# Joint of the output stage and the second MLP: group two's first 24 products placed in the gap, a group's two feature blocks multiplied first and both ReLUs after, the last cast later

## Chip, core and metric

The kernel runs on one core of one Trainium2 chip. The metric is the device time of one execution in microseconds, as the median of several runs. A core has five engines with a queue each, and each queue is worked off in order: TensorE (PE, with its weight loads shown apart as PEld), VectorE (DVE), ScalarE (ACT), GpSimd (POOL) and SyncE (SP), which issues the DMAs. An instruction waits until the instructions of other engines that it depends on have signalled; whatever stands behind it in its queue waits with it.

## What is computed

Two layers over 512 latent tokens and 256 context tokens of width 1024. Each layer is a token mixer (pooling in the first, grouped-query attention in the second) and then a squared-ReLU MLP with 4096 hidden features. The change lies where the attention of layer two ends and its MLP begins, on latent tokens alone:

```python
y_lat = attention(...) @ w_o
x = x + gt1 * rms_norm(y_lat, g_mix_post)
h = rms_norm(x, g_mlp_pre) * (1.0 + sc2) + sh2
m = jnp.square(jax.nn.relu(h @ w_in)) @ w_out      # w_in 1024 x 4096, w_out 4096 x 1024
x = x + gt2 * rms_norm(m, g_mlp_post)
```

## The kernel before

Every fp32 operand of a product is split into a high part (a cast to the matmul's format, on ACT) and a low part (source minus high part, on DVE). A product is then three matmuls: high by high, high by low, low by high. "A product" below means one such matmul instruction on PE; 128 rows of the depth of 1024 are called a step `k`, so that one block of 128 hidden features over some tokens takes 8 steps of 3 products, 24 in all.

**Output stage** (`output`). It multiplies the attention's result by `w_o` for four tiles of 128 tokens, each in two column halves (`attn_mm`, PSUM tiles `psy`, L1302). `attn_ev` multiplies the result by the gate (DVE, L326) and takes the mean square (ACT, L170); POOL turns it into a reciprocal root (`rstd`, L183 and L185); `norm_r` adds the residual (DVE, L329); `norm_s` takes the mean square of the new rows (ACT, L170, then POOL L177 and L185) and `norm_c` scales them (ACT L526 or DVE L528). When two tiles are scaled, `norm_pair` (`modulated_pair`) transposes them on PE (L350, PSUM tiles `psx`), modulates them (DVE L358, ACT L361) and splits them into `h1H` in `ra` and `h1L` in `unit[0]`, which is part of `rb`. The first pair (tiles 0 and 1) is split in two pieces of four steps `k` each (ACT L369, DVE L370), the second pair (tiles 2 and 3) in four pieces of two steps (ACT L364, DVE L365). The stage also computes the last gate from `w_ada` on DVE (`ada_sum`, L268 to L277).

**Second MLP** (`mlp1`). The 4096 hidden features are worked in 16 groups of 256; here they are counted one to sixteen, while the code counts `g` from 0. `Inner.part(c, f, ks)` issues the products (L567) of feature block `f` (0 or 1) of a group for the token chunk `c` and the steps `ks`, into a PSUM tile `psin` taken from the pool `psA`, which has two buffers of two banks each. `squares` multiplies a block, takes its ReLU and then its square (ACT L578 and L912), block after block. Of two groups each the squares are combined and multiplied by `w_out` in seven products of sums, a fast scheme (`product`, PSUM tiles `pso` from the pool `psB`, L921); the weight sums and the operands are made by `put` and `both` (ACT L893, DVE L893 and L899).

Group one is already joined to the output stage before the change: the token half of the first pair (chunk 0, 24 products per block, 256 tokens wide) is multiplied inside `output`, the other half in `mlp1`. Its blocks take one `psA` buffer each, with one bank per token half. Group two is multiplied in `mlp1` in 48 products that are 512 tokens wide; its weights are loaded during the output stage and split whole (ACT L142, DVE L145) at the start of `mlp1`.

**What sets the order.** The steps of `output` carry a due time (`at(time, function, ...)`) and are issued in the order of these times; the framework then schedules the instructions of each engine by its own timing model, except for those that are pinned with `keep_in_program_order`. So the place of an instruction in a queue follows from the due times and from that model together. The loads of weights go through three buffers `raw` (pool `rawp`): a load is issued when an earlier content of a buffer has been read for the last time.

## Time and profile before

| | us |
|---|---|
| median of 3 runs | 1172.9 (1172.45 to 1174.26) |
| the profiled execution | 1173.48 |
| its span on the core | 1171.7 |
| PE busy in the span | 1143.0 |
| DVE busy | 938.4 |
| ACT busy | 636.7 |
| POOL busy | 67.0 |

The span is what the profile covers; the execution took 1.8 us more. A row of the timeline gives start, duration, engine, line, operation, output and inputs with their shapes, and in brackets how long the engine had been idle and what ended that. Matmuls overlap in the array, so a row's duration (0.28 us for one that is 256 wide) is longer than the distance to the next one. Rows that follow each other with the same text are merged, with their number behind an x. Times are counted from the start of the span.

### The profile page before, as it was taken

To read this page: it belongs to the slowest core of one execution; us is meant where nothing else is said; L and a number is where in the kernel's file an instruction comes from. 1 tells how busy PE (TensorE), PEld (TensorE's weight loads), DVE (VectorE), ACT (ScalarE), POOL (GpSimd) and SP (SyncE) were. 2 spreads that over 40 slices of the span, in tenths; PEclk is the share of its full clock that TensorE was granted. 3 is DMA by queue.
4 is the path that set the end of the run, shared out by engine and by line. 5 is a ranking of instruction groups with operands and counts; after the bars stand their busy time and mean duration, and the time that the engine had idled before them with its cause. 6 is when DMAs were issued, how large, how long until landed. Compare 5 with 4: busy or idle time off the path is not lost.

```text
span 1171.7 us, 15966 instructions
## 1 busy us (share of the span) xinstructions
PE 1143.0 (98%) x6172; PEld 989.2 (84%) x6172; DVE 938.4 (80%) x1538; ACT 636.7 (54%) x1082; POOL 67.0 (6%) x120
## 2 busy tenths in 40 slices
PE   7899999999999999999999999999899999999997
PEld 5579899889899988998887889988888888888886
DVE  4688687989988997996778599877787779778876
ACT  4577655555454534555675388852776436535522
POOL 2030000000000000000241200001100000000001
PEclk9899999999999999999999999999999999999999
DMA  9884213343334334343423101115234124314312
GB/s 375 354 318 154 72 45 135 133 159 109 144 144 144 144 137 147 112 144 108 180 73 107 37 1 37 37 73 197 91 138 150 61 84 144 108 36 144 108 37 107
DMA packets 25516, 147.32 MB, mean 126 GB/s; under 512 B 2785, under 2 KB 5217, under 8 KB 9698
## 3 DMA queue, kind: packets, MB, share of 16 engines
q1 hardware_dynamic: 25442, 146.32, 34.2%
q8 instruction: 48, 0.79, 0.3%
q14 instruction: 26, 0.21, 0.1%
HBM read 138.96 MB, written 7.34 MB: 125 GB/s over the span
## 4 chain that ended last, share of the span: by engine, by line
PE 49%; issue 42%; POOL 3%; DVE 2%; ACT 2%; DMA 1%; SPq 0%; POOLq 0%; DVEq 0%; ACTq 0%
PE pso L817 22%; PE psin L691 18%; PE psin L567 3%; PE psq L1064 2%; PE pspool L65 1%; POOL rs L185 1%; PE psada L65 1%; PE pspool L490 1%; POOL rs L1073 1%; DMA raw<-in_w_ada 1%; DMA xr<-in_x 1%; PE psada L227 1%; POOL ms L183 1%; DVE ra L65 0%; ACT junk L170 0%
## 5 line engine op out<-in xcount | busy, mean ns | idle before, releaser
L817 PE MATMUL pso<-units,rb 128*128 128x512 f32 x1152 | 278.2, 392 | 0.0
L817 PEld LDWEIGHTS pso<-units,rb 128*128 128x128 f32 x1152 | 214.8, 188 | 41.2
L273 DVE SCALAR_TENSOR_TENSOR rows<-raw,cond,rows 128x256 f32<-128x256 f32 x280 | 126.5, 475 | 2.0
L829 DVE TENSOR_TENSOR acc<-acc,pso 128x512 f32<-128x512 f32 x129 | 85.1, 674 | 41.4 <-PE pso L817 41.2
L567 PE MATMUL psin<-ra,rb 128*128 128x512 f32 (+1 forms) x432 | 103.3, 340 | 1.8 <-ACT ra L364 1.6
L921 PE MATMUL pso<-units,pairs 128*128 128x512 f32 x336 | 82.3, 389 | 0.0
L567 PE MATMUL psin<-ra 128*128 128x512 f32 x256 | 80.5, 390 | 0.0
L567 PEld LDWEIGHTS psin<-ra,rb 128*128 128x128 f32 x432 | 69.9, 189 | 11.3 <-ACT ra L364 1.9
L921 PEld LDWEIGHTS pso<-units,pairs 128*128 128x128 f32 x336 | 63.1, 188 | 13.1
L925 DVE TENSOR_TENSOR acc<-acc,pso 128x512 f32<-128x512 f32 x72 | 48.7, 681 | 28.8 <-PE pso L921 28.8
L183 POOL TENSOR_SCALAR ms<-ss 128x1 f32<-128x1 f32 x20 | 11.4, 572 | 998.3 <-ACT junk L170 946.1
L691 PE MATMUL psin<-ra,units 128*128 128x384 f32 x336 | 65.5, 337 | 0.4 <-ACT psin L703 0.4
L691 PE MATMUL psin<-sums,units 128*128 128x384 f32 x336 | 63.9, 337 | 0.0
L691 PEld LDWEIGHTS psin<-ra,units 128*128 128x128 f32 x336 | 59.7, 188 | 3.9 <-ACT psin L703 0.9
L691 PEld LDWEIGHTS psin<-sums,units 128*128 128x128 f32 x336 | 58.9, 188 | 1.7
L145 DVE TENSOR_TENSOR units<-raw,units 128x1024 fp32r<-128x1024 f32 (+2 forms) x49 | 55.1, 1148 | 4.5 <-ACT units L142 4.4
L567 PEld LDWEIGHTS psin<-ra 128*128 128x128 f32 x256 | 48.0, 188 | 10.0
L142 ACT CAST units<-raw 128x1024 fp32r<-128x1024 f32 (+2 forms) x49 | 46.8, 994 | 14.0 <-PE pso L817 10.2
L827 ACT COPY acc<-pso 128x512 f32<-128x512 f32 x48 | 27.2, 588 | 48.9 <-PE pso L817 48.6
L567 PE MATMUL psin<-rb 128*128 128x512 f32 (+1 forms) x144 | 52.6, 367 | 0.2 <-DVE rb L365 0.2
L1064 PE MATMUL psq<-units,ra 128*128 128x512 f32 x216 | 51.7, 392 | 0.0
L567 PE MATMUL psin<-rb,ra 128*128 128x512 f32 x128 | 49.8, 389 | 0.0
(279 smaller groups left out, 2346.7 us busy)
## 6 DMA issues: line engine op xcount, KB each, us to landing
raw<-in_w_ada SPq DMA_DIRECT2D x48, 1024.0 KB, 4.9
raw<-in_w_mlp_in SPq DMA_DIRECT2D x32, 1024.0 KB, 4.9
raw<-in_w_mlp_out SPq DMA_DIRECT2D x32, 1024.0 KB, 5.3
raw<-in_w_qkv SPq DMA_DIRECT2D x6, 1024.0 KB, 4.8
spill<-xr SPq DMA_DIRECT2D x10, 512.0 KB, 4.2
xr<-spill SPq DMA_DIRECT2D x10, 512.0 KB, 6.8
raw<-in_w_o SPq DMA_DIRECT2D x4, 1024.0 KB, 4.8
xr<-in_x SPq DMA_DIRECT2D x4, 512.0 KB, 5.2
```

What stands on the lines that cost most here:

```text
L65: return lambda *args, **kw: self.tc.keep_in_program_order(f(*args, **kw))
L142: a = sc.copy(hi, raw)
L145: b = ve.tensor_tensor(out=lo, in0=raw, in1=hi, op=ALU.subtract)
L273: ve.scalar_tensor_tensor(out=r, in0=raw[:, k, :], scalar=cond[:, k, c:c + 1], in1=r, op0=ALU.mult, op1=ALU.add)
L567: te.matmul(ps[:, bank, o:o + ln], w[:, k, fs], rhs, start=start, stop=(k == KT - 1 and n == 2), skip_group_check=len(ks) < KT)
L691: te.matmul(bank, w[k], a[k], start=start and k == 0 and m == 0, stop=stop and k == 3 and m == 2, skip_group_check=True)
L817: te.matmul(pss[h][:, 0:cols[h][1]], a[:, f, ts_], w[:, f, cols[h][0]:sum(cols[h])], start=(n == 0 and not seeded[t]), stop=(n == len(seq) ...
L827: sc.copy(d, ps)
L829: ve.tensor_tensor(out=d, in0=d, in1=ps[:, 0:w], op=ALU.add)
L921: te.matmul(ps, a, w, start=(m == 0), stop=(m == len(seq) - 1))
L925: ve.tensor_tensor(out=M[n][:, t], in0=M[n][:, t], in1=ps, op=ALU.add)
L1064: te.matmul(ps, a[:, k, sl], w[:, k % 4, :], start=(k == 0 and n == 0), stop=(k == KT - 1 and n == 2))
```

## The change

Five things change together.

1. *Both blocks of groups one and two share one PSUM buffer* (`paired`): block `f` takes bank `f`, and the two token halves lie beside each other in that bank. Group one then holds one of the two `psA` buffers, and group two can take the other one while group one is still being multiplied.
2. *Group two is multiplied in token halves of 256.* The 24 products of its first block over the first half (`first1[1].part(0, 0, ...)`, due at 47.5 and 47.6) are issued in the output stage.
3. *Its weights are split in halves.* The raw weights were loaded in the output stage before, too. Now the first block's half is cast and subtracted there (`half_early`, due at 36, L1339 and L1340) into `rb[4096:6144]`, and the second block's half at the start of `mlp1`.
4. *`squares` of a paired group* issues the products of both blocks that are still open, and then the two ReLUs and squares.
5. *The last cast of the first token pair* (steps 4 to 7) with its subtraction leaves `modulated_pair` and becomes `upper_half`, due at 41.65 (L1386 and L1387), with the cast pinned. Group one's products on that half are issued in pieces of four steps.

```diff
-    def modulated_pair(t, i, s, hi, lo, works, wide, fine, on_act):
+    def modulated_pair(t, i, s, hi, lo, works, wide, fine, on_act, late=None):
...
                 h = works[q // 2].rearrange("p (k n) -> p k n", n=256)
+                if late is not None and q == 3:
+                    late.append((place(hi, ks), place(lo, ks), h))
+                    continue
                 sc.copy(place(hi, ks), h)
                 ve.tensor_tensor(out=place(lo, ks), in0=h, in1=place(hi, ks), op=ALU.subtract)
...
     def chunks1(g):
-        if g == 0:
-            return [[(0, 0, 0, 256)], [(1, 0, 256, 256)]], [(0, 2, 256, 0)]
+        if g < 2:
+            return [[(0, 0, 0, 256)], [(0, 256, 256, 256)]], [(0, 1, 512, 0)]
         return [[(0, 0, 0, 512)]], [(0, 1, 512, 0)]
...
         def part(self, c, f, ks=range(KT)):
             (wH, wL), (aH, aL) = self.w, self.a
-            if f not in self.ps:
+            if self.paired and not self.ps:
+                t = psA.tile([P, 2, 512], F32, tag="a", name="psin")
+                self.ps = {q: t[:, q:q + 1, :] for q in range(2)}
+            elif f not in self.ps:
                 self.ps[f] = psA.tile([P, 2, 512], F32, tag="a", name="psin")
+            if self.f0 and f == 0:
+                wH, wL = self.f0
...
         def squares(inner, q):
+            for f in range(2) if inner.paired else ():
+                for c in range(2):
+                    if (c, f) not in begun[inner]:
+                        inner.part(c, f)
             for f in range(2):
-                inner.part(len(inner.chunks) - 1, f)
+                if not inner.paired:
+                    inner.part(0, f)
                 sc.activation(F[:, q, f, :], inner.relu(f), AF.Square)
...
-        wi = [None, w_in(1, 1, ins[1], True)]
+        wi = [None, None]
+        hi, lo = (ra[:, z:z + 2048] for z in (0, 2048))
+        hi, lo = (z.rearrange("p (k n) -> p k n", n=256) for z in (hi, lo))
+        put((hi[:, :, P:], lo[:, :, P:]), raw1[0][:, :, P:], True)
+        second.w = hi, lo
+        begun = {inner: ((0, 0), (0, 1)), second: ((0, 0),)}
...
-            a12, a22 = squares(inner_of(2 * p + 1), 1)
+            a12, a22 = squares(inner_of(2 * p + 1) if p else second, 1)
...
+    def half_early():
+        hi, lo = (rb[:, z:z + 1024].rearrange("p (k n) -> p k n", n=P) for z in (4096, 5120))
+        sc.copy(hi, raw1[0][:, :, 0:P])
+        ve.tensor_tensor(out=lo, in0=raw1[0][:, :, 0:P], in1=hi, op=ALU.subtract)
+        first1.append(Inner(1, (None, None), h1H, h1L, None, chunks1, LAT, True, (hi, lo)))
...
+        def upper_half():
+            hi, lo, h = halves[0]
+            tc.keep_in_program_order(sc.copy(hi, h))
+            ve.tensor_tensor(out=lo, in0=h, in1=hi, op=ALU.subtract)
+
+        at(41.65, upper_half)
         for f in range(2):
-            at((41, 42)[f], lambda *a: first1[0].part(*a), 0, f)
+            for h in range(2):
+                at(41.7 + f / 10 + h, lambda *a: first1[0].part(*a), 0, f, range(4 * h, 4 * h + 4))
...
+        at(26, lambda: raw1.append(raw_load(w_mlp_in[1, 1], rawp).rearrange("p (k n) -> p k n", n=256)))
+        at(36, half_early)
+        for h in range(2):
+            at((47.5, 47.6)[h], lambda ks: first1[1].part(0, 0, ks), range(4 * h, 4 * h + 4))
```

The engines' queues before and after show what the scheduler made of it. On PE, at the place where the second token pair is transposed (tiles `psx_7592` to `psx_7607`), group one's blocks are `psin_7525` and `psin_7559` before. The end of the first token half and the beginning of the second read:

```order
L567 MATMUL psin_7559<-ra_99,rb_100 128x256 x2
L567 MATMUL psin_7559<-rb_100 128x256
L567 MATMUL psin_7559<-ra_99,rb_100 128x256
L350 MATMUL psx_7592<-ident_87,acc_86 128x128 x3
L350 MATMUL psx_7597<-ident_87,acc_86 128x128 x3
L350 MATMUL psx_7602<-ident_87,acc_86 128x128 x3
L350 MATMUL psx_7607<-ident_87,acc_86 128x128 x3
L567 MATMUL psin_7525<-ra_99,rb_100 128x256
L567 MATMUL psin_7559<-ra_99,rb_100 128x256
L567 MATMUL psin_7525<-rb_100 128x256
```

Now, with group one in `psin_7538` and group two in `psin_7631`:

```order
L577 MATMUL psin_7631<-rb_100 128x256
L577 MATMUL psin_7631<-ra_99,rb_100 128x256 x2
L350 MATMUL psx_7595<-ident_87,acc_86 128x128 x3
L350 MATMUL psx_7600<-ident_87,acc_86 128x128 x3
L350 MATMUL psx_7605<-ident_87,acc_86 128x128 x3
L350 MATMUL psx_7610<-ident_87,acc_86 128x128 x3
L577 MATMUL psin_7631<-rb_100 128x256
L577 MATMUL psin_7631<-ra_99,rb_100 128x256
L577 MATMUL psin_7538<-ra_99,rb_100 128x256
L577 MATMUL psin_7631<-ra_99,rb_100 128x256
L577 MATMUL psin_7538<-rb_100 128x256
```

Between the end of the `psy` products and these twelve transposes stood 48 products of group one; now 48 of group one and 22 of group two stand there, and the last 2 of group two's 24 come behind the transposes. From there to the end of group two stood 48 products that are 256 wide and 48 that are 512 wide; now 74 and 48, all 256 wide.

Earlier in that stretch, where the three parts of group one meet group two's start, PE now has group two's first twelve products ahead of group one's steps 4 to 7, which need the late cast and its subtraction:

```order
L577 MATMUL psin_7631<-ra_99,rb_100 128x256 x2
L577 MATMUL psin_7631<-rb_100 128x256
L577 MATMUL psin_7538<-ra_99,rb_100 128x256
L577 MATMUL psin_7631<-ra_99,rb_100 128x256 x2
L577 MATMUL psin_7538<-rb_100 128x256
L577 MATMUL psin_7538<-ra_99,rb_100 128x256 x2
```

The first `psin_7538` row here is the first product that waits for the late cast, the second is the first that waits for its subtraction; before the change the same products stood behind 24 of group one.

On DVE, from the first subtraction of the first pair to the modulation of the second pair, before:

```order
L370 TENSOR_TENSOR rb<-acc,ra 128x4x256
L358 TENSOR_SCALAR acc<-psx,avec_96,mods_92 128x256
L326 TENSOR_TENSOR acc<-psy,gate 128x256
L370 TENSOR_TENSOR rb<-acc,ra 128x4x256
L329 SCALAR_TENSOR_TENSOR xr<-acc,rs,xr 128x1024
L528 TENSOR_SCALAR acc<-xr,rs 128x1024
```

and now:

```order
L373 TENSOR_TENSOR rb<-acc,ra 128x4x256
L358 TENSOR_SCALAR acc<-psx,avec_96,mods_92 128x256
L326 TENSOR_TENSOR acc<-psy,gate 128x256
L329 SCALAR_TENSOR_TENSOR xr<-acc,rs,xr 128x1024
L1387 TENSOR_TENSOR rb<-acc,ra 128x4x256
L531 TENSOR_SCALAR acc<-xr,rs 128x1024
```

The late subtraction has moved behind the residual of the last token tile (L329).

More of the change, by code (lines that the diff above doesn't have):

```diff
@@ L528, in norm_c, with norm_pair @@
             ve.tensor_scalar(out=accv[:, t, :], in0=xr[:, t, :], scalar1=r, scalar2=None, op0=ALU.mult)
-    def norm_pair(t, i, s, hi, lo, wide, fine, on_act):
-        modulated_pair(t, i, s, hi, lo, [accv[:, t, :], accv[:, t + 1, :]], wide, fine, on_act)
+    def norm_pair(t, i, s, hi, lo, wide, fine, on_act, late=None):
+        modulated_pair(t, i, s, hi, lo, [accv[:, t, :], accv[:, t + 1, :]], wide, fine, on_act, late)
     def chunks0(g):
@@ L545, in backbone, with __init__ @@
     class Inner:
-        def __init__(self, g, w, aH, aL, hid, chunks_of, ntok):
-            self.w, self.a, self.ntok = w, (aH, aL), ntok
+        def __init__(self, g, w, aH, aL, hid, chunks_of, ntok, paired=False, f0=None):
+            self.w, self.a, self.ntok, self.paired, self.f0 = w, (aH, aL), ntok, paired, f0
             self.hid = hid and [z.rearrange("p (f n) -> p f n", n=ntok) for z in hid]
@@ L566, in part @@
                             rhs = a[:, k, t0:t0 + ln]
+                            start = start and not (self.paired and (f, bank) in self.opened)
+                            self.opened.add((f, bank))
                         te.matmul(ps[:, bank, o:o + ln], w[:, k, fs], rhs, start=start,
-                                  stop=(k == KT - 1 and n == 2), skip_group_check=len(ks) < KT)
+                                  stop=(k == KT - 1 and n == 2), skip_group_check=len(ks) < KT or self.paired)
         def relu(self, f):
@@ L868, in mlp0, with mlp1 @@
         finish(0, [part, (NG - 1, inner.hid, wo_)], order, last)
-    def mlp1(inner, last):
+    def mlp1(inner, second, last):
         nonlocal xr, gate, junk
@@ L1313, in attn_ev @@
             rs[t] = rstd(ss1[t], 1 + len(ps1[t]))
-    first1 = []
+    first1, raw1 = [], []
+    def half_early():
[3 more added lines that the diff above has]
+        first1.append(Inner(1, (None, None), h1H, h1L, None, chunks1, LAT, True, (hi, lo)))
     def attention(st, base, unit_t):
@@ L1344, in output @@
     def output(st, base):
-        at = lambda i, fn, *args: st.at(base + i, fn, *args)
+        at, halves = lambda i, fn, *args: st.at(base + i, fn, *args), []
         for n, (ch, t) in enumerate(((0, 0), (0, 1), (1, 0), (0, 2), (1, 1), (0, 3), (1, 2), (1, 3))):
@@ L1355, in output @@
                     at(36.3 if t == 1 else 47.4, norm_pair, t - 1, 1, 1, h1H, h1L, t == 1, t == 3,
-                       ((False, True, True, False, True, False, True, False), (True, False, True, False, True, False, True, False))[t // 2])
+                       ((False, True, True, False, True, False, True, False), (True, False, True, False, True, False, True, False))[t // 2], halves if t == 1 else None)
+        def upper_half():
[3 more added lines that the diff above has]
+        at(41.65, upper_half)
         for f in range(2):
-            at((41, 42)[f], lambda *a: first1[0].part(*a), 0, f)
+            for h in range(2):
+                at(41.7 + f / 10 + h, lambda *a: first1[0].part(*a), 0, f, range(4 * h, 4 * h + 4))
         parts[1] = small.tile([P, 32], F32, tag="part", name="part", bufs=1)
@@ L1362, in output @@
         raws = []
-        at(20, lambda: first1.append(Inner(0, w_in(1, 0, early, False, raws), h1H, h1L, None, chunks1, LAT)))
+        at(20, lambda: first1.append(Inner(0, w_in(1, 0, early, False, raws), h1H, h1L, None, chunks1, LAT, True)))
         at(32, lambda: split(*raws[0]))
+        at(26, lambda: raw1.append(raw_load(w_mlp_in[1, 1], rawp).rearrange("p (k n) -> p k n", n=256)))
+        at(36, half_early)
+        for h in range(2):
+            at((47.5, 47.6)[h], lambda ks: first1[1].part(0, 0, ks), range(4 * h, 4 * h + 4))
     def fin_b(t):
@@ L1378, in backbone @@
     mlp0(first[0], hids0, (4, 5, 0, 1, 2, 3), extra0, mid0, last0, before0)
-    mlp1(first1[0], last1)
+    mlp1(*first1, last1)
 _INS = ["x", "ctx", "w_ada", "w_pool", "pool_scale", "w_qkv", "g_q", "g_k", "w_o", "w_mlp_in", "w_mlp_out"]
```

## Prediction

> **What bounds the kernel now.** I read the page's busy shares first, then the busy time by stretches around the change, then who PE waited for there, then the timeline of the same place. The page and the stretches:

> ```profile
> PE 1143.0 (98%) x6172; PEld 989.2 (84%) x6172; DVE 938.4 (80%) x1538; ACT 636.7 (54%) x1082; POOL 67.0 (6%) x120
> core 0: us, PE busy (x) PEld busy (x) DVE busy (x) ACT busy (x) POOL busy (x), PEclk, DMA share, GB/s
> 827.20:835.20 8.00, 6.47 (x55) 6.27 (x53) 4.12 (x6) 3.16 (x6) 2.37 (x5) 1.00 0.17 68
> 835.20:844.80 9.60, 7.66 (x61) 7.17 (x61) 7.50 (x11) 7.46 (x12) 0.00 (x0) 1.00 0.00 1
> 844.80:855.80 11.00, 11.00 (x50) 9.11 (x49) 10.50 (x11) 7.76 (x10) 0.00 (x0) 1.00 0.51 167
> 880.00:1150.00 270.00, 270.00 (x1198) 223.27 (x1198) 213.53 (x252) 125.94 (x160) 0.00 (x0) 1.00 0.28 98
> PE psin L567 <- ACT ra L364: 1.6, 1, 1.6
> PE psx L350 <- DVE acc L528: 1.6, 1, 1.6
> PE psin L567 <- DVE rb L365: 0.2, 1, 0.2
> ```

> PE is busy for 98% of the span. Behind the joint it never stops: 11.00 of 11.00 us, later 270.00 of 270.00, at a granted clock of 1.00. So what PE saves at the joint reaches the end whole, as long as no new wait arises behind it. At the joint PE idles 1.53 us of the first 8.00 and 1.94 of the next 9.60, and the last three rows name the waits. This is PE's timeline there:

> ```profile
> 827.29 0.28 PE L567 MATMUL psin<-ra,rb 128*128 128x256 f32 x1
> 833.39 0.28 PE L567 MATMUL psin<-ra,rb 128*128 128x256 f32 x1
> 835.28 1.53 PE L350 MATMUL psx<-ident,acc 128*128 128x128 f32 x12 [1.60 <-DVE acc L528]
> 838.44 0.50 PE L567 MATMUL psin<-ra,rb 128*128 128x256 f32 x2 [1.64 <-ACT ra L364]
> 839.17 0.39 PE L567 MATMUL psin<-rb 128*128 128x256 f32 x1 [0.22 <-DVE rb L365]
> 844.79 0.50 PE L567 MATMUL psin<-ra 128*128 128x512 f32 x1
> 855.81 5.60 PE L921 MATMUL pso<-ra,pairs 128*128 128x512 f32 x24
> ```

> From 827.29 PE works on group one's first token half. After its last product at 833.39 it stands until 835.28, because the second token pair is not scaled yet: gap one. Twelve transposes follow, then gap two until that pair is modulated, cast (838.44) and subtracted (839.17). Then 46 products take until 844.79 and group two's 48 wide ones until 855.81. From the start of the transposes to the end of group two it is 855.81 - 835.28 = 20.53 us, and to the second product behind gap two 839.17 - 835.28 = 3.89 us.

> **Prices on PE.** 46 products that are 256 wide take 844.79 - 839.17 = 5.62 us, 0.122 each. 48 that are 512 wide take 855.81 - 844.79 = 11.02, 0.230 each; two narrow ones do the same work in 0.244. Cutting group two into halves therefore costs 96 x 0.122 - 11.02 = 0.69 us of PE's time, with nothing to hide it. Ahead of gap one, 48 products and 4 transposes took 833.51 - 827.29 = 6.22 us, taking 0.12 for the last; with 0.11 for a transpose (12 in 1.53 less the drain) a product is 0.120 there.

> **Gap one: 70 products in place of 48.** 22 of group two's 24 products come before the twelve transposes. They bring 22 x 0.120 = 2.64 us of work to a gap of 833.51 to 835.28, 1.77 us. The excess delays the transposes, and with them everything of gap two. Without any further wait they would start at 835.28 + 2.64 - 1.77 = 836.15. Whether there is one depends on two chains. These are the rows of the first pair's split and of the last tile's root:

> ```profile
> 821.58 0.30 POOL L183 TENSOR_SCALAR ms<-ss 128x1 f32<-128x1 f32 x1 [5.85 <-ACT junk L170]
> 821.70 0.55 DVE L358 TENSOR_SCALAR acc<-psx,avec,mods 128x256 f32<-128x256 f32 x1 [1.00 <-PE psx L350]
> 822.28 1.48 ACT L361 ACTIVATE acc<-psx,mods,avec 128x256 f32<-128x256 f32 x3 [0.80 <-DVE acc L358]
> 823.94 1.06 ACT L170 ACTIVATE junk<-xr 128x1024 bf16<-128x1024 f32 x1 [0.18 <-DVE xr L329]
> 826.06 1.23 DVE L370 TENSOR_TENSOR rb<-acc,ra 128x1024 fp32r<-128x1024 f32 x1 [0.97 <-ACT ra L369]
> 827.66 0.41 DVE L326 TENSOR_TENSOR acc<-psy,gate 128x256 f32<-128x256 f32 x1
> 827.79 1.04 ACT L369 CAST ra<-acc 128x1024 fp32r<-128x1024 f32 x1
> 828.73 0.39 ACT L170 ACTIVATE junk<-psy 128x256 bf16<-128x256 f32 x1
> 828.87 1.23 DVE L370 TENSOR_TENSOR rb<-acc,ra 128x1024 fp32r<-128x1024 f32 x1 [0.79 <-ACT ra L369]
> 829.01 0.20 ACT L170 ACTIVATION_READ_ACCUMULATOR junk<-psy 128x1 f32 x1
> 829.39 0.88 POOL L183 TENSOR_SCALAR ms<-ss 128x1 f32<-128x1 f32 x1 [2.04 <-ACT junk L170]
> 830.94 1.28 DVE L329 SCALAR_TENSOR_TENSOR xr<-acc,rs,xr 128x1024 f32<-128x1024 f32 x1 [0.85 <-POOL rs L185]
> 834.47 0.75 DVE L528 TENSOR_SCALAR acc<-xr,rs 128x1024 f32<-128x1024 f32 x1 [2.24 <-POOL rs L185]
> ```

> *The start.* Four `psy` products slip ahead of the first pair's transposes (10 in place of 6). The modulation at 821.70 waited for those, so it comes 4 x 0.12 = 0.48 later. ACT had 0.18 us to spare ahead of 823.94, so its cast and the subtraction of 826.06 come 0.30 later and end at 827.59. PE's second product, the first to read a low part, now waits about 0.27 us for it. Bounds: 0 if the modulation were not late, 0.48 if ACT's slack is none; I take 0.27.

> *The last cast later.* The cast of 827.79 stood ahead of the last mean square at 828.73. Now this square waits only for DVE's gate product (827.66, 0.30 later, ending near 828.4), starts near 828.45 and has its sum at 828.95, not 829.21: 0.26 earlier. POOL's step at 829.39 took 0.88 us, the same step at 821.58 only 0.30. In the first case DVE was in the subtraction of 828.87 until 830.10, in the other it was idle. That subtraction now stands behind the residual, so DVE is idle again, and I take 0.30. The residual then starts at 830.94 - 0.26 - 0.58 = 830.10; by the other bound, 0.88, at 830.68. [...]

> *The late subtraction behind the residual.* DVE does it after the residual (1.28, less the overlap of rows): from 831.3 to 832.55, or from 831.9 to 833.1 by the other bound. PE meets its first use after 24 products of group one, three transposes, 11 of group two, a transpose and three more: 827.29 + 0.27 + 38 x 0.120 + 4 x 0.11 = 832.56. So PE waits 0.0 us, at most 0.6. The scaling of the last tile ends 4.28 us after the residual's start (830.94 to 835.22), at 834.4 or 834.95, and DVE is free for it: no wait for the transposes any more.

> The transposes then start at 836.15 + 0.27 = 836.42, at most 837.0.

> **Gap two.** Nothing in it is shortened: modulation, cast and subtraction still follow the transposes, so the second product behind comes 3.89 us after them. PE has four products to put in, where it had two (two left over of group two's first half; and one each of the two groups at the cast). From there 118 remain: 74 of the token halves and 48 of group two's second block, less those four. That is 118 x 0.122 = 14.40 us. Group two ends at 836.42 + 3.89 + 14.40 = 854.71, against 855.81: 1.10 us earlier. The ends: 1.39 with neither wait, 0.52 with the late one.

> **The early half of the weights.** It adds a cast and a subtraction of 1024 columns in the output stage; such ones took 1.05 and 1.22 us (first two rows):

> ```profile
> 841.64 1.05 ACT L893 CAST ra<-raw 128x1024 fp32r<-128x1024 f32 x1
> 843.99 1.22 DVE L893 TENSOR_TENSOR ra<-raw,ra 128x1024 fp32r<-128x1024 f32 x1
> 800.95 0.33 SPq L123 DMA_DIRECT2D raw<-in_w_mlp_in  x1
> 812.24 1.29 DVE L329 SCALAR_TENSOR_TENSOR xr<-acc,rs,xr 128x1024 f32<-128x1024 f32 x1 [0.46 <-POOL rs L185]
> 815.96 1.14 ACT L526 ACTIVATE acc<-xr,rs 128x1024 f32<-128x1024 f32 x1
> 820.74 1.69 PE L350 MATMUL psx<-ident,acc 128*128 128x128 f32 x14
> ```

> The load is the one issued at 800.95, which keeps its place on SP. The cast and the subtraction stand ahead of rows of ACT and DVE that lead to the residual of 812.24. If nothing covered them there, this would come 1.05 + 1.22 = 2.27 us later, and so would the scaling of that tile, which ended at 817.10 (815.96 and 1.14). Its first use is the transposes at 820.74: 3.64 us of cover, so I cost the early half at nothing. A load that lands over 1.4 us late would use the cover up, and its price is the time beyond. At the start of `mlp1` a cast and a subtraction of 8x128 replace ones of 2048; no row shows that strided form, and between the 1.05 of 1024 columns and the 1.91 of 2048 I take the first, its own count. Group two's second block needs them 9 us after their issue, so either is hidden.

> **Behind the joint.** Both ReLUs now come after all products, and the cast of group three's weights stands ahead of them on ACT. Group one's last product falls near 836.42 + 3.89 + 63 x 0.122 = 848.0, and only then may its weights be overwritten. The cast (1.9, as at 870.84 below) and a subtraction of 2.3 make group three's weights ready near 852.6, 2 us before PE gets there; the two ReLUs, two squares and a cast of some 0.6 each bring the first operand of `w_out` near 854.1, with 8 of group three's products ahead of its use. The thinnest place is the load of group four's weights:

> ```profile
> 861.40 0.60 ACT L578 ACTIVATE work<-psin 128x512 f32<-128x512 f32 x1
> 866.10 9.33 SPq L123 DMA_DIRECT2D raw<-in_w_mlp_in  x2
> 870.84 1.91 ACT L142 CAST ra<-raw 128x2048 fp32r<-128x2048 f32 x1 [0.39 <-DMA raw<-in_w_mlp_in]
> 873.60 1.06 ACT L923 COPY acc<-pso 128x512 f32<-128x512 f32 x2
> DMA to landing us min/median/max: 4.7/5.3/7.9
> ```

> It waits for a buffer whose last reader stands behind group two's second ReLU (861.40 before). That ReLU now follows the weight cast, group one's two ReLUs and squares and the weight sums, and I estimate it 1.7 us later; so the issue is at 867.8 and the cast, 4.74 us after the issue as before, near 872.6. Behind it ACT makes a square, a cast and then the copies (873.60 before) that free PSUM for the fifth product with `w_out`: about 876.7, where PE arrives at 877.25. So 0.55 us is left and it costs nothing.

> **Sum.** Gap one is filled whole, 1.77 us, and gap two by two products, 0.24; the narrow products cost 0.69 and the start 0.27. That is 1.05, and 1.10 by the walk along the queue above; I take 1.1. The profiled execution would go from 1173.48 to 1172.4. The median of the runs is 0.58 below the profiled execution, so 1172.9 becomes 1171.8. The measurement can tell about 0.2%, 2.35 us, from no change; this is less.

> **Rivals.**

> *PE waits for the late subtraction.* If POOL's step stays at 0.88 us or the residual is late for another reason, group one's second part stops PE by up to 0.6 us: 1172.4. For it speaks that the subtraction is queued behind an instruction that waits for POOL; against it, that DVE is idle then.

> *Both gaps are filled.* If the transposes did not have to wait for the 22 products, all 24 would be hidden: 24 x 0.12 = 2.88 less 0.69 is 2.19 us, 1170.7. The queue speaks against it, since PE takes the products first. More than that the moved work can't give, so a gain of over 2.35 us needs something that this profile doesn't show.

> *Slower: the fifth product waits for PSUM.* Place: ACT's cast of group four's weights. Landings in this stretch took 4.7 to 7.9 us (last row). At 7.9 the copies come 3.2 us later, of which 0.55 is covered: 2.65 of wait, 1.55 more than the gain, 1174.5. It turns the sign from a slip of 1.65 us on. Against it: the load of 866.10 landed in 4.7, with nothing beside it.

> *The change moves nothing.* The gain would be eaten where narrow products cost as much as the gap gives: 1172.9. That needs both waits at their bounds and 0.5 us more.

> **Chances.** The forecast, 0.9 to 1.4 us of gain: 0.45. The late subtraction, 0.3 to 0.9: 0.18. Both gaps filled: 0.07. No change: 0.04. A wait for PSUM or another one behind the joint: 0.15, of which 0.12 over 0.2%, since one such wait draws others with it. A gain of over 0.2% by something that I have not seen: 0.11. So faster by over 0.2% has 0.11, within it 0.45 + 0.18 + 0.07 + 0.04 + 0.03 = 0.77, slower 0.12. The time is that of the likeliest, 1171.8. The range goes from 1170.2, which takes in both gaps filled, to 1174.2, which takes in most of the PSUM wait.

> **What would show it.** PE's twelve transposes of the second pair start near 836.4 and nothing waits for the scaling of the last tile; PE's wait ahead of the second token half stays at 1.6 us; the wait for the late subtraction is under 0.6; POOL's step takes 0.3; group two ends near 854.7; behind it PE is busy without a break until 1150. The forecast is wrong if the transposes come near 835.3, if PE waits for ACT or POOL ahead of 833 for more than 0.6, or if PE idles between 855 and 900.

## The result, and the profile after

| | before | after |
|---|---|---|
| median of 20 executions each, us | 1173.68 (1172.45 to 1175.37) | 1171.52 (1169.53 to 1173.67) |
| ratio of the times | | 0.9983, 95% interval 0.9977 to 0.9989 |
| the profiled execution, us | 1173.48 | 1171.59 |
| its span, us | 1171.7 | 1169.8 |

The changed kernel is 0.17% faster, 2.0 us with an interval of 1.3 to 2.7. That is less than the 0.2% from which the prediction counts a change, though the interval doesn't reach 1. A second set (the first experiment below) gave 0.9988, 0.9979 to 0.9997, that is 1.4 us; one of its eleven executions of the changed kernel took 2883.2 us and is left out of the ratio.

The stretches of the prediction in the profile after (busy time of each engine, then the granted clock of PE, the DMA share and GB/s), and all waits of PE from 820 to 1140:

```profile
827.20:835.20 8.00, 8.00 (x68) 8.00 (x68) 3.67 (x5) 2.88 (x6) 1.65 (x4) 1.00 0.17 68
835.20:844.80 9.60, 7.98 (x66) 7.57 (x65) 7.83 (x11) 5.98 (x10) 0.00 (x0) 1.00 0.12 22
844.80:855.80 11.00, 11.00 (x87) 10.66 (x86) 8.68 (x9) 8.04 (x10) 0.00 (x0) 1.00 0.46 170
880.00:1150.00 270.00, 270.00 (x1199) 223.36 (x1198) 213.63 (x253) 126.24 (x160) 0.86 (x2) 1.00 0.27 98
PE psin L577 <- ACT ra L364: 1.4, 1, 1.4
PE psin L577 <- DVE rb L365: 0.2, 1, 0.2
```

The first stretch, in which PE idled 1.53 us before, has no gap any more: the wait of 1.6 us for the scaling of the last tile is gone. The second still idles 1.62 us, and behind it PE never stops. PE's timeline at the same place:

```profile
819.26 0.38 PE L350 MATMUL psx<-ident,acc 128*128 128x128 f32 x2
826.74 0.28 PE L577 MATMUL psin<-ra,rb 128*128 128x256 f32 x1
826.97 0.39 PE L577 MATMUL psin<-rb 128*128 128x256 f32 x1
831.94 0.35 PE L577 MATMUL psin<-rb 128*128 128x256 f32 x1
835.83 1.47 PE L350 MATMUL psx<-ident,acc 128*128 128x128 f32 x12
838.94 0.51 PE L577 MATMUL psin<-ra,rb 128*128 128x256 f32 x2 [1.40 <-ACT ra L364]
839.66 0.39 PE L577 MATMUL psin<-rb 128*128 128x256 f32 x1 [0.22 <-DVE rb L365]
853.91 0.40 PE L577 MATMUL psin<-ra,rb 128*128 128x512 f32 x1
1139.94 1.52 PE L827 MATMUL pso<-ra,units 128*128 128x512 f32 x6
```

The first and the last row give a measure that the start of the program can't disturb: from the first transposes of the first token pair to the first output product of the last group. I call it the joint's stretch. It takes 1139.94 - 819.26 = 320.68 us here. In the profile of before the same rows are these:

```profile
819.81 0.38 PE L350 MATMUL psx<-ident,acc 128*128 128x128 f32 x2
1141.82 1.52 PE L817 MATMUL pso<-ra,units 128*128 128x512 f32 x6
```

That is 322.01 us, so the change is worth 1.33 us on the joint's stretch. The other 0.55 us between the two profiles lie ahead of 819. Of the change only the early half of the weights stands there (its cast is at 808.16), and the listed waits of PE between 700 and 819 are the same. PE's clock lost 2.95 us there in the profile of before and 1.49 in the one after, so I don't count this part as the change's.

### The profile page after: what moved, and what is told of

Read it like the earlier page. It is cut to its first block, busy times and chain, and to the rows that moved or that the text cites. A ratio compares the mean times of both kernels' runs of the same rounds, so it can differ in the third digit from the quotient of the medians.

```text
span 1169.8 us, 16065 instructions
## 1 busy us (share of the span) xinstructions
PE 1143.4 (98%) x6220; PEld 991.0 (85%) x6220; DVE 938.6 (80%) x1539; ACT 636.7 (54%) x1083; POOL 65.6 (6%) x120
## 4 chain that ended last, share of the span: by engine, by line
PE 57%; issue 31%; DVE 4%; ACT 3%; POOL 2%; DMA 2%; SPq 0%; POOLq 0%; DVEq 0%; ACTq 0%
PE pso L827 22%; PE psin L701 18%; PE psy L1322 3%; PE psin L577 3%; PE po L1296 2%; PE psq L1084 2%; PE pss L1257 2%; DMA raw<-in_w_ada 1%; PE psada L65 1%; PE pspool L493 1%; PE pspool L65 1%; POOL rs L1093 1%; POOL rs L185 1%; DVE sm L1261 1%; PE pspt L1282 1%
## 5 line engine op out<-in xcount | busy, mean ns | idle before, releaser
L577 PE MATMUL psin<-ra,rb 128*128 128x256 f32 (+1 forms) x464 | 109.3, 336 | 1.5 <-ACT ra L364 1.4
L577 PEld LDWEIGHTS psin<-ra,rb 128*128 128x128 f32 x464 | 74.9, 189 | 11.0 <-ACT ra L364 1.6
L577 PE MATMUL psin<-ra 128*128 128x512 f32 (+1 forms) x256 | 76.5, 376 | 0.0
L183 POOL TENSOR_SCALAR ms<-ss 128x1 f32<-128x1 f32 x20 | 9.1, 453 | 996.5 <-ACT junk L170 942.9
L577 PE MATMUL psin<-rb 128*128 128x512 f32 (+1 forms) x160 | 57.3, 359 | 0.2 <-DVE rb L365 0.2
L142 ACT CAST units<-raw 128x1024 fp32r<-128x1024 f32 (+2 forms) x49 | 46.7, 994 | 14.3 <-PE pso L827 10.4
L577 PE MATMUL psin<-rb,ra 128*128 128x512 f32 (+1 forms) x128 | 48.1, 376 | 0.0
```

The source lines that it names most:

```text
L142: a = sc.copy(hi, raw)
L577: te.matmul(ps[:, bank, o:o + ln], w[:, k, fs], rhs, start=start, stop=(k == KT - 1 and n == 2), skip_group_check=len(ks) < KT or self.paired)
```

## Experiments

All kernels compute the same result. The edits are against the changed kernel. They ran in three sets (e1 to e4, e5 to e8, e9 and e10), each with executions of the kernel before beside it; a ratio is to those. Where TensorE's order is "held", the products or transposes named are kept in the order in which the code issues them; without that the planner orders them itself. Each row below has the joint's stretch, PE's waits in it as the profile lists them, and what PE's clock lost there (busy time times one minus the granted clock, added over stretches of 2 us).

| kernel | stretch | waits of PE | lost to the clock | stretch less both |
|---|---|---|---|---|
| before | 322.01 | 1.60 + 1.64 + 0.22 | 0 | 318.55 |
| e7, before again | 323.48 | 1.60 + 1.64 + 0.23 | 1.62 | 318.39 |
| after | 320.68 | 1.40 + 0.22 | 0 | 319.06 |
| e1, after again | 320.70 | 1.40 + 0.22 | 0 | 319.08 |
| e2, cast early | 322.39 | 1.64 + 0.23 | 1.59 | 318.93 |
| e3, no fill | 322.82 | 1.79 + 1.07 + 0.35 | 0 | 319.61 |
| e4, 9 ahead and 15 behind | 322.34 | 1.79 | 1.65 | 318.90 |
| e5, 12 and 12 | 319.50 | 0.36 | 0 | 319.14 |
| e6, cast early, 18 and 6 | 319.75 | 0.36 + 0.22 | 0 | 319.17 |
| e9, as e5, one block wide | 319.18 | 0.36 | 0 | 318.82 |
| e10, each ReLU at once | 324.31 | 1.40 + 0.22 + 2.37 + 0.58 | 0 | 319.74 |

The last column is the point of the table. For kernels with the changed kernel's narrow products it is 318.9 to 319.2 in all but two rows, so waits and clock explain the stretch. e3 and e10, which have the most waits of these kernels, lie 0.55 and 0.68 us above the changed kernel. Part of that is how a wait is counted: from the modelled end of the last product, some 0.16 us after the next one could have started (the prediction's gap of 1.77 us is listed as 1.60), so each further wait adds about as much to this column. The rest stays unexplained. A wait under 0.15 us is not listed: e3, e5 and e9 have one more of 0.08 to 0.14.

**e1, the changed kernel again.**

> The changed kernel once more, untouched, as the yardstick of the other three. From the first transposes of the first pair of token tiles (819.26 in the profile after, 819.81 in that of before) to the first output product of the last group (1139.94 and 1141.82) it should again take 320.7 us +-0.15, against 322.0 before: a gain of 1.35 us at the joint. If the rest of the measured 2.0 us is chance in the start of the program (0.55 us in the two profiles, ahead of anything that the change touches), the first transposes of this run fall anywhere between 819.2 and 819.9; if the change itself makes the start earlier, they fall at 819.3 again.

Measured: 320.70, so 1.3 us of gain at the joint repeat to 0.02. The first transposes came at 818.86, which is neither of the two profiles' times: the start varies from execution to execution, and the last section says with what. The times were 1172.11 against 1173.28.

**e2, the late cast undone.**

```diff
-                       ((False, ...), (True, ...))[t // 2], halves if t == 1 else None)
+                       ((False, ...), (True, ...))[t // 2])
...
-        at(41.65, upper_half)
```

> Only the late cast is undone: the last cast and subtraction of the first pair stand with the other three again. Theory (the 24 products alone cover the wait): POOL's step L183 grows back from 0.30 to 0.8-0.9 us, the last scaling L531 ends about 0.6 to 1.0 us later (834.3 to 834.7 on the clock of the profile after), still ahead of 835.83, where TensorE comes to the second pair's transposes; so no wait appears, and first transposes to last group take 320.7 +-0.2: the time of the changed kernel within 0.2 us. Rival (the late cast carries the gain): a wait on L531 of 0.6 to 1.0 us ahead of the transposes, and a time above the changed kernel's by as much.

The rows of its profile:

```profile
828.66 0.87 POOL L183 TENSOR_SCALAR ms<-ss 128x1 f32<-128x1 f32 x1 [2.04 <-ACT junk L170]
833.73 0.75 DVE L531 TENSOR_SCALAR acc<-xr,rs 128x1024 f32<-128x1024 f32 x1 [2.24 <-POOL rs L185]
835.68 1.47 PE L350 MATMUL psx<-ident,acc 128*128 128x128 f32 x12
840.00:842.00 2.00, 2.00 (x11) 2.00 (x11) 2.00 (x4) 2.00 (x3) 0.00 (x0) 0.50 0.00 0
```

POOL's step is back at 0.87 us and the scaling ends later, at 834.48, but that is still 1.2 us ahead of the transposes, which wait for nothing. So the 24 products alone close the first gap, as the theory had it. The stretch itself came out at 322.39, not 320.7, and the last row shows why: PE's granted clock was at 0.50 for a while behind the remaining wait, which cost 1.59 us in this execution. Over 11 executions the time was 1171.57, ratio to before 0.9992 (0.9982 to 1.0002), which can't be told from the changed kernel's 0.9988 in the same set.

**e3, no products in the gap.**

```diff
-        for h in range(2):
-            at((47.5, 47.6)[h], lambda ks: first1[1].part(0, 0, ks), range(4 * h, 4 * h + 4))
-        begun = {inner: ((0, 0), (0, 1)), second: ((0, 0),)}
+        begun = {inner: ((0, 0), (0, 1)), second: ()}
```

with the second pair's transposes and the products of groups one and two in the order that the expectation names.

> The second pair's transposes and the products of groups one and two are held in the order of before: 48 products of group one, 16 transposes, 48 of group one, then all of group two; the late cast and the 256-wide products stay. Theory by the prediction (the wait of 1.77 us ahead of the transposes does not depend on the cast): both waits come back whole, 1.77 + 1.64 + 0.22 us against 1.62 after; first transposes to last group 322.7, that is 2.0 us over the changed kernel and 0.7 (the narrow products) over before. Theory by the profile after (L531 already ended at 833.70, that is 1.0 us earlier than before, since the late cast cleared its way): the first wait is only about 1.0 us, waits in all about 2.6, first transposes to last group 321.7, 1.0 us over the changed kernel and 0.3 under before.

Measured: 322.82 on the stretch, ratio to before 1.0011 (1.0002 to 1.0020). Its waits:

```profile
PE psin L577 <- DVE rb L1387: 1.8, 1, 1.8
PE psin L577 <- ACT ra L364: 1.1, 1, 1.1
PE psin L577 <- DVE rb L365: 0.3, 1, 0.3
```

The first theory's 322.7 is met by luck: neither expectation named the first row, and no wait for the scaling is left, which both had. Without group two's products between the lower and the upper half of group one's, PE comes to the upper half while DVE is still at the residual, and waits 1.79 us for the late subtraction. So the late cast is free only behind the products of group two. With before, after and e2 this makes a square of PE's waits:

| waits of PE, us | cast early | cast late |
|---|---|---|
| 24 products behind | 3.46 (before) | 3.21 (e3) |
| 24 products ahead | 1.87 (e2) | 1.62 (after) |

The products take 1.59 us of wait away in either column, the late cast 0.25 in either line. The square compares sums alone: in e3 the waits stand at other places than in before, so that the differences agree to 0.01 us is in part chance.

**e4, 9 of the 24 products ahead of the transposes and 15 behind.**

```diff
-        for h in range(2):
-            at((47.5, 47.6)[h], lambda ks: first1[1].part(0, 0, ks), range(4 * h, 4 * h + 4))
+        at(47.3, lambda: first1[1].part(0, 0, range(0, 3), True))
+        at(47.5, lambda: first1[1].part(0, 0, range(3, KT), True))
```

> Of the 24 products only 9 are held ahead of the second pair's transposes and 15 right behind them (in the changed kernel 22 stand ahead of the last 12 transposes and 2 behind). By the profile after, L531 ends at 833.70, and TensorE has done 52 products by then; with 57 ahead it comes to the transposes at about 833.8 without a wait, 2.0 us earlier than in the changed kernel. The first cast of the second pair (L364) follows the transposes' start by the same 3.1 us, so to 836.9, and the 15 products (1.8 us) behind the transposes keep TensorE busy until 837.5. Theory (what is left in the joint is the wait behind the transposes, 1.40 + 0.22 us, and only it): both waits go, first transposes to last group 319.1, 1.6 us under the changed kernel, which beats both kernels. Rival (the next operand is late at once: group three's weights or the first operand of its output product): a new wait of 0.8 to 1.6 us between 851 and 856, and at most 0.8 us under the changed kernel.

A miss: 322.34, and 1171.83 us, ratio 0.9989 (0.9980 to 0.9998). The wait behind the transposes went, as expected, but with the order held group one's upper half again stood directly behind its lower half. Its one wait and the clock behind it:

```profile
830.42 0.39 PE L577 MATMUL psin<-rb 128*128 128x256 f32 x1 [1.79 <-DVE rb L1387]
832.00:834.00 2.00, 2.00 (x11) 2.00 (x11) 0.22 (x1) 0.00 (x0) 0.00 (x0) 0.50 0.00 0
```

**e5, twelve between group one's halves and twelve behind the transposes.** Both lessons together: 12 products of group two cover the late subtraction, 12 the cast of the second pair.

```diff
-                at(41.7 + f / 10 + h, lambda *a: first1[0].part(*a), 0, f, range(4 * h, 4 * h + 4))
+                at(41.7 + f / 10 + h, lambda *a: first1[0].part(*a), 0, f, range(4 * h, 4 * h + 4), True)
-        for h in range(2):
-            at((47.5, 47.6)[h], lambda ks: first1[1].part(0, 0, ks), range(4 * h, 4 * h + 4))
+        at(42.5, lambda: first1[1].part(0, 0, range(0, 4), True))
+        at(47.5, lambda: first1[1].part(0, 0, range(4, KT), True))
```

> The changed kernel with its late cast, but TensorE's order at the joint held: 24 products of group one on the lower half of the features, 12 of group two on the same half, 24 of group one on the upper half, the second pair's 16 transposes, 12 of group two. On the clock of the profile after, TensorE reaches the upper half at 831.2 and the late subtraction L1387 ends at 831.84, so a wait of 0.65 us is left there; the transposes start at 834.7, behind L531 (833.70), and the first cast of the second pair comes 3.1 us later, at 837.8, when the 12 products behind the transposes have carried TensorE to 838.1. Theory (the joint is worth what TensorE waits in it, plus what its clock loses where a wait of 1.6 us or more makes the granted clock fall to 0.5): one wait of 0.65 instead of 1.40 + 0.22 and no fall of the clock; first transposes of the first pair to the last group's first output product 319.7 +-0.2 us against 320.7. Rival (some later operand is the limit): 320.4 or more, with a new wait between 850 and 862.

Measured: 319.50, and 1170.67 us, ratio to before 0.9976 (0.9967 to 0.9985). One listed wait is left in the whole stretch:

```profile
831.73 0.39 PE L577 MATMUL psin<-rb 128*128 128x256 f32 x1 [0.36 <-DVE rb L1387]
834.60 1.91 PE L350 MATMUL psx<-ident,acc 128*128 128x128 f32 x16
838.30 0.38 PE L577 MATMUL psin<-rb 128*128 128x256 f32 x1
```

The transposes start 15.5 us after the first ones (834.60 - 819.09), in the changed kernel 16.6 (835.83 - 819.26), and the wait for the second pair has all but closed: ahead of the product at 838.30 PE idles for 0.13 us.

**e6, cast early, 18 products ahead and 6 behind.** The edits of e2, and e4's with the border at `range(0, 6)`.

> All casts of the first pair early, as before the change, and TensorE's order held: 48 products of group one, 18 of group two, 16 transposes, 6 of group two. In the run with the early cast alone L531 ended 15.57 us after the first transposes of the first pair; 66 products carry TensorE to just that point, so no wait ahead of the transposes. The first cast of the second pair comes 3.1 us after their start, the 16 transposes and 6 products take 2.7 us: a wait of about 0.4, and 0.2 for the subtraction. Theory as above: waits of 0.6 us in all, no fall of the clock, 319.7 +-0.2 us on the same stretch. Rival (the clock falls whatever the wait, about as often as not): 1.3 to 1.7 us more, with granted clock 0.5 in a stretch of about 3 us.

Measured: 319.75, and 1170.72 us, ratio 0.9978 (0.9969 to 0.9987). The waits are 0.36 and 0.22, the clock stayed at 1.00. So without the late cast the joint can be nearly as short, if the transposes come as soon as the scaling is done (here at 836.72, right behind its end at 836.70).

**e7, the kernel before again.**

> The kernel before, untouched, for a second profile. Theory (its joint is 322.0 us by its three waits of 1.60, 1.64 and 0.22, and the spread of its times comes from the granted clock at the start): 322.0 +-0.2 where the clock stays at 1.00 in the joint, 1.3 to 1.7 more where it falls there; the first transposes at about 817.3 plus what the clock loses in the first 50 us (2.95 us in the first profile, which had them at 819.81).

Measured: 323.48 on the stretch with the same three waits. The first transposes came at 817.92; the clock had lost nothing ahead of them, and 817.3 was expected for that. Its stretches around the second wait:

```profile
836.00:838.00 2.00, 1.24 (x6) 1.04 (x7) 2.00 (x5) 2.00 (x5) 0.00 (x0) 0.89 0.01 4
838.00:840.00 2.00, 2.00 (x12) 2.00 (x11) 1.14 (x3) 2.00 (x3) 0.00 (x0) 0.50 0.00 0
840.00:842.00 2.00, 2.00 (x15) 2.00 (x15) 2.00 (x1) 0.79 (x1) 0.00 (x0) 0.76 0.00 0
```

The clock fell in the joint and cost 0.14 + 1.00 + 0.48 = 1.62 us. The stretch is 1.47 us longer than the first profile's, so the two agree to 0.15.

**e8, narrow products everywhere.** This multiplies the price of the narrow products by 14: 672 pairs in place of 48.

```diff
-        return [[(0, 0, 0, 512)]], [(0, 1, 512, 0)]
+        return [[(0, 0, 0, 256), (1, 0, 256, 256)]], [(0, 2, 256, 0)]
```

> The changed kernel with all products of groups three to sixteen 256 wide too: 1,344 narrow ones in place of 672 wide ones, the rest the same. Prediction's price (0.122 each against 0.230): 672 x 0.0144 = 9.7 us more on the stretch from the first transposes to the last group, so 330.4. By the durations that the profile after shows (0.120 and 0.2285): 672 x 0.0115 = 7.7 us more, 328.4. If narrow products cost nothing (rival: the array is the bound, twice 256 columns as long as 512): 320.7.

Measured: 1149.60 - 819.13 = 330.47 us, 9.79 over the changed kernel's 320.68, with the same two waits and the clock at 1.00. So two narrow products cost 9.79 / 672 = 0.0146 us more than one wide one, and the 48 pairs of group two 0.70.

**e9, e5 with group two's second block wide.**

On top of the edits of e5:

```diff
-                for c in range(2):
+                for c in range(1 if inner is second and f else 2):
-                    for bank, o, t0, ln in self.chunks[c]:
+                    for bank, o, t0, ln in [(0, 0, 0, 512)] if self.f0 and f else self.chunks[c]:
```

> The held order of the twelve-and-twelve kernel, and group two's second feature block is multiplied 512 wide: 24 wide products in place of 48 narrow ones. Price of a narrow pair by the run with all narrow products: 9.8 us / 672 = 0.0146 us, so 24 x 0.0146 = 0.35 us less, if nothing waits: first transposes to last group 319.15 +-0.15 against 319.50. Rival (the wide block needs both halves of the second pair, and TensorE has 24 products fewer to go on with while its casts come in four pieces): a wait on the casts between 838 and 843, and 319.5 or more.

Measured: 319.18, as expected, and 1170.28 us, ratio to before 0.9973 (0.9962 to 0.9983). On the stretch this is the shortest kernel of the study: 1.50 us under the changed kernel and 2.83 under the one before. By the times alone it can't be told from e5 or e6.

**e10, each ReLU behind its own block.**

```diff
-            for f in range(2) if inner.paired else ():
-                for c in range(2):
-                    if (c, f) not in begun[inner]:
-                        inner.part(c, f)
             for f in range(2):
-                if not inner.paired:
-                    inner.part(0, f)
+                for c in range(2 if inner.paired else 1):
+                    if not inner.paired or (c, f) not in begun[inner]:
+                        inner.part(c, f)
```

> The changed kernel with one part undone: the ReLU of a group's first feature block follows that block's products at once, ahead of the second block's, in groups one and two. Theory (both ReLUs lie beside the products of group two, on an engine that TensorE does not wait for there): first transposes to last group 320.7 +-0.2, as in the changed kernel. Rival (the order of the ReLUs carries some of the gain, by when it lets group three's weights and first output operand come): 0.3 us or more away from it, and a wait of TensorE between 850 and 862.

The largest miss: 324.31, 3.6 us over the changed kernel. The rows:

```profile
846.34 1.90 ACT L142 CAST rb<-raw 128x2048 fp32r<-128x2048 f32 x1 [0.55 <-PE psin L577]
848.15 0.59 ACT L588 ACTIVATE work<-psin 128x512 f32<-128x512 f32 x1
848.79 0.50 PE L577 MATMUL psin<-ra,rb 128*128 128x512 f32 x1 [2.37 <-ACT work L588]
850.10 1.20 PE L936 MATMUL pso<-ra,pairs 128*128 128x512 f32 x4 [0.58 <-ACT pairs L903]
859.53 0.28 PE L577 MATMUL psin<-ra 128*128 128x256 f32 x1
```

A group's two blocks share one PSUM buffer. With a ReLU between them the second block's products wait for the first block's ReLU, since the program orders a write into a buffer behind a read of it. The planner therefore moved group two's second block back to 859.53, behind group three's first products and the products with `w_out`. Those came too early: group three's first one (848.79) needed a PSUM buffer that group one's second ReLU had to free, and that stood behind the weight cast on ACT. In the changed kernel group two's second block stands at that place, from 848.15 to 853.91. The rows show the waits and the order; that the shared buffer is why the planner moved the block I read from the program, and no run tests it by itself. Nor does a run undo the early half of the weights alone.

## Why the prediction was right

The forecast was 1171.8 us and a gain of 1.1 us. Measured are 1171.52 us, and 1.33 on the joint's stretch. That the median came so close to the forecast is in part luck. The forecast took 1.1 us from 1172.9, the median of 3 executions; 20 gave 1173.68, and from there it would have been 1172.6. The medians lie 2.16 us apart, about twice the forecast gain; the second set has 1.4, and the first set's interval, 1.3 to 2.7 us, still takes in the 1.33 of the trace. What was right is the mechanism at the joint, in its main terms. To compare clocks, add 0.55 us to the profile after (first transposes 819.81 against 819.26).

**Prices on PE.** 0.69 us for the narrow products was forecast; e8 gives 0.70.

**Gap one.** It was to be filled whole, with the transposes at 836.42. They came at 835.83 + 0.55 = 836.38 and waited for nothing.

**The last cast later.** These rows of the profile after answer to the ones of before:

```profile
828.16 1.04 ACT L1386 CAST ra<-acc 128x1024 fp32r<-128x1024 f32 x1
828.44 0.30 POOL L183 TENSOR_SCALAR ms<-ss 128x1 f32<-128x1 f32 x1 [1.48 <-ACT junk L170]
829.42 1.28 DVE L329 SCALAR_TENSOR_TENSOR xr<-acc,rs,xr 128x1024 f32<-128x1024 f32 x1 [1.72 <-POOL rs L185]
830.62 1.22 DVE L1387 TENSOR_TENSOR rb<-acc,ra 128x1024 fp32r<-128x1024 f32 x1
832.95 0.75 DVE L531 TENSOR_SCALAR acc<-xr,rs 128x1024 f32<-128x1024 f32 x1 [1.11 <-POOL rs L185]
```

POOL's step took the 0.30 us forecast. Over all profiles it took 0.30 in the eight kernels with the late cast and 0.87 or 0.88 in the four with the early one (before, e2, e6, e7), where DVE's subtraction runs beside it (828.87 to 830.10 in the profile of before). In the profile after DVE stood idle for 1.72 us, up to 829.42, and the step lies in that time. That the subtraction is what makes the step longer was the author's estimate from such rows; no run tests it by itself. (In its row at 821.58 DVE was not idle to the end of the step, as the prediction reads it: a modulation, which reads `psx`, began at 821.70, and the step still took 0.30.) The residual began at 829.97 on the clock of before (830.10 forecast), and the late subtraction ended at 832.39 (832.55). PE's first use of it came at 831.94, 0.10 us behind its end, with no wait, as forecast. The prediction called this a wait of 0.0, at most 0.6. It didn't say how much hangs on the products of group two that stand ahead: e3 and e4, without them, paid 1.79 there.

**The start.** 0.27 us was forecast for PE's second product; the rows at 826.74 and 826.97 stand 0.23 apart, and 0.12 is the usual distance, so it was 0.11. This term was too large by 0.16; with the end that the prediction works out for the subtraction and that product's start in the profile of before (827.41) it would be 827.59 - 827.41 = 0.18.

**Gap two.** The second product behind it was forecast 3.89 us after the transposes' start, and came 839.66 - 835.83 = 3.83 after. The wait in it was 1.40. That is the 1.64 less the 0.24 that the prediction's sum takes for the two added products; its list of signs, which has this wait stay at 1.6, contradicts that sum and was wrong. The 118 products behind it took 853.91 - 839.66 = 14.25 us, 0.121 each, against 14.40. So group two ended at 854.46 on the clock of before, against 854.71 forecast. Of these 0.25 us 0.04 had come up to the transposes, 0.06 came in gap two and 0.15 in the products behind it. With the terms as measured the sum is 1.77 + 0.24 - 0.70 - 0.11 = 1.20 us; no run assigns the other 0.13 of the 1.33.

**The early half of the weights.** It was costed at nothing, with 3.64 us of cover:

```profile
808.16 1.05 ACT L1339 CAST rb<-raw 128x1024 fp32r<-128x1024 f32 x1 [3.01 <-DMA raw<-in_w_mlp_in]
813.90 1.28 DVE L329 SCALAR_TENSOR_TENSOR xr<-acc,rs,xr 128x1024 f32<-128x1024 f32 x1 [0.45 <-POOL rs L185]
817.42 1.15 ACT L529 ACTIVATE acc<-xr,rs 128x1024 f32<-128x1024 f32 x1 [0.18 <-POOL rs L185]
```

ACT even stood 3.01 us for the load, and the scaling ended at 818.57, or 819.12 on the clock of before, against 817.10. The transposes that use it began at 820.66. So of the cover 2.1 us were left.

**Behind the joint.** Group three's weights were to be ready near 852.6 and the first operand of `w_out` near 854.1. They were ready at 852.3 and 853.5 on the clock of before, from the ends of these rows:

```profile
849.48 2.29 DVE L145 TENSOR_TENSOR rb<-raw,rb 128x2048 fp32r<-128x2048 f32 x1 [1.09 <-ACT rb L142]
852.29 0.68 DVE L903 TENSOR_TENSOR pairs<-hid,pairs 128x512 fp32r<-128x512 f32 x1
```

Group four's load was issued at 867.31 on that clock and its cast began at 872.18 (867.8 and 872.6 forecast); the copies behind it, forecast to free PSUM at about 876.7, ran from 875.46 to 876.52. PE was busy without a break from there on, so the slower rival, a wait for PSUM, did not come.

**Where the reasoning fell short.** *Both gaps are filled* was set at 1170.7 and rejected because PE takes the 22 products ahead of the transposes. That was right for the kernel given. But nothing except this order stood against it: the scaling had ended at 833.70 in the profile after, 2.1 us before the transposes, and by then PE had done all but about 18 of the products ahead of them. The prediction named the order and did not say that another one would gain. e5, which holds twelve of the products back, is 1.18 us shorter on the stretch than the changed kernel.

## What to carry to other kernels

When work is put into a gap, ask when the waiting work becomes ready, not how long the gap was: put in only as many products as fit until then, and the rest behind it, where the next gap is. Work that covers one wait can cover a second that was never visible; e3 and e10 each took one part of the change out and met a wait that no profile of the complete kernel shows. And to weigh 1 us in 1170, measure a stretch between two fixed instructions in the trace, add up its waits, and look at the granted clock in it, before any median.

## What the runs showed of the hardware

```profile
38.00:40.00 2.00, 1.30 (x24) 0.56 (x24) 2.00 (x5) 0.00 (x0) 0.00 (x0) 0.85 0.98 393
40.00:42.00 2.00, 1.30 (x6) 1.33 (x7) 0.78 (x4) 1.15 (x3) 0.00 (x0) 0.50 1.04 430
42.00:44.00 2.00, 2.00 (x11) 2.00 (x11) 1.21 (x3) 1.79 (x5) 0.00 (x0) 0.50 0.99 410
44.00:46.00 2.00, 2.00 (x11) 1.86 (x9) 0.98 (x2) 0.00 (x0) 0.00 (x0) 0.50 0.15 61
46.00:48.00 2.00, 2.00 (x18) 0.46 (x17) 0.00 (x0) 0.00 (x0) 0.00 (x0) 0.95 0.00 0
```

```profile
26.00:28.00 2.00, 1.04 (x8) 0.18 (x8) 0.09 (x1) 0.00 (x0) 0.00 (x0) 0.76 1.01 422
28.00:30.00 2.00, 2.00 (x11) 1.20 (x6) 0.72 (x1) 0.00 (x0) 0.00 (x0) 0.50 1.02 426
30.00:32.00 2.00, 2.00 (x30) 1.29 (x29) 0.41 (x3) 0.50 (x1) 0.00 (x0) 0.88 1.00 418
```

From the means, half clock lasted 0.96 + 2.00 + 0.48 = 3.44 us after, and 0.44 + 2.00 + 0.96 = 3.40 in the joint of e7. Before it was 0.60 + 6.00 + 0.20 = 6.80, twice as long. In the joint the clock fell behind a wait of 1.64 us (e2), behind waits of 1.60 and 1.64 with the transposes between them (e7) and behind one of 1.79 (e4). It stayed at 1.00 behind 1.60 and 1.64 in the first profile of before, behind 1.79 (e3) and behind 2.37 (e10), so a wait of 1.6 us or more, as the expectation of e5 has it, was not always followed by a fall. In the six profiles whose longest wait was 1.40 or less it never fell in the joint.

In the seven profiles that have changes of the clock far apart, these lie on a grid. Read in stretches of 0.01 us, the clock of the profile after fell at 27.053, came back at 30.466, which is 3.413 us of half clock, and fell again at 1167.104, behind PE's last work. From the return to that fall it is 1136.638 us, 333 times 3.4133. In the profile of before the return at 46.208 and the last fall at 1169.193 lie 1122.985 us apart, 329 times that length. In five more profiles two falls can be placed from the means over 2 us: they lie 798.72 us (e2), 1129.80 (e3), 334.52 (e4) and 1123.00 (e5 and e9) apart, which is 234, 331, 98 and 329 times 3.4133, each to 0.02 us. Cut into pieces of that length from a fall or a return on, the joints of e2, e4 and e7 have these pieces ahead of their falls, and last comes the piece with the least work in the first profile of before (the first number behind the comma is PE's busy time):

```profile
836.13:839.55 3.42, 1.56 (x13) 1.12 (x11) 2.75 (x6) 3.35 (x7) 0.00 (x0) 1.00 0.01 2
827.93:831.34 3.41, 1.62 (x13) 1.41 (x13) 2.42 (x2) 1.15 (x2) 0.69 (x2) 1.00 0.38 153
834.13:837.54 3.41, 1.55 (x12) 1.11 (x10) 2.98 (x6) 3.41 (x8) 0.00 (x0) 1.00 0.01 2
834.69:838.10 3.41, 1.53 (x12) 1.29 (x12) 2.17 (x5) 2.24 (x5) 0.00 (x0) 1.00 0.00 0
```

In every other piece of the joints PE was busy for 1.81 us or more, and the clock did not fall behind it; this leaves out e10, whose clock stayed at 1.00 up to 1166 us, so that no change of it places its pieces. A border of the grid cuts e3's wait of 1.79 into 0.70 and 1.09; e4's 1.79 lies in one piece whole. So a wait of the same length was followed by a fall in one run and not in the other, and I take its place on the grid for the reason. Three falls are few, though, and the last row does not fit a limit on busy time alone: the clock stayed up behind it, and no run shows why.

One such fall of a single length costs 1.4 to 1.7 us by the measure of the table, as much as the whole change. At the start it explains most of the spread: the first transposes lay between 817.26 and 821.11 us over the twelve profiles, and between 816.9 and 818.1 when the time lost to the clock ahead of them is taken off. Among the 20 executions of the changed kernel the span goes from 1167.7 us at a mean granted clock of 0.999 to 1171.9 at 0.994.
